# A hybrid retention and attention block: weight slabs requested one at a time, casts chained, one v-stage low half and the output pieces moved

## The chip, the cores and the metric

The kernel runs on one core of a Trainium2 chip. The metric is device time in microseconds (us) for one execution of the whole program. Engines are named as in the profile: PE multiplies matrices (PEld loads its weights), DVE and ACT work element by element, POOL does so too, SP issues most DMA transfers. Each engine runs its instructions in the order in which they stand; between engines and DMA queues, semaphores hold an instruction back until its data and its buffer are ready.

## The reference, cut to what matters

One layer over x of 1024 rows and 1024 columns, all in float32:

```python
h = rms_norm(x, ln1_g)
rq, rk, rv, rg, aq, ak, av, gate_a, gate_b = split(h @ w_in + b_in)

# A: retention, 4 heads, q and k of 128, v of 256, chunks of 128
ry = head_group_norm(retention_chunkwise(rotary(rq), rotary(rk), rv))
branch_a = (silu(rg) * ry) @ w_ret_out

# B: attention in a window of 128, 16 query heads of 64, 2 key heads, sinks
ay = sliding_window_sink_attention(rotary(aq), rotary(ak), av, sinks)
branch_b = ay @ w_attn_out

merged = sigmoid(gate_a) * branch_a + sigmoid(gate_b) * branch_b
x = x + merged @ w_out
h2 = rms_norm(x, ln2_g)
x = x + (silu(h2 @ w_gate) * (h2 @ w_up)) @ w_down
out = rms_norm(x, lnf_g)
```

The change touches how three parts of this are fed: the columns of `w_in` for `aq` and the gates, those for `rv`, and `ay` on its way to `w_attn_out`.

## The kernel before, in words

Every float32 product is done as three products of halves. A **high half** is a cast on ACT (`nc.scalar.copy`), the **low half** is what the cast leaves out, a subtraction on DVE; PE adds high×high, high×low and low×high in one PSUM bank. `split` (L132) makes both halves, its two instructions stand at L133 (ACT) and L136 (DVE). A weight so takes a way of four steps: a DMA brings a raw slab, ACT casts it, DVE subtracts, PE multiplies.

The program runs in stages, one after the other on PE: norm and keys and values of the attention (to about 43 us), the **units stage** (43 to 343), the **v stage** (343 to 423), the w stage (423 to 616), retention with the output projections, and the feed-forward part.

In the **units stage** the attention runs as 32 units: unit u is quad g = u // 8 (four query heads) and block b = u % 8 of 128 rows. The loop at L630 takes in each turn the transposes of unit i−2 (`u_transpose`), the scores of unit i (`u_scores`), some steps of filler products, and the values of unit i−2 (`u_values`). Scores go to a ring of two PSUM banks (`s`, two heads each); ACT copies one half of a bank to SBUF (L521), DVE puts the other half in (`copy_predicated`, L522) and takes the minimum (L524), and ACT does the exponentials (L532). The transposed probabilities are split into `ph` (ACT, L550) and `pl` (DVE, L551), from which DVE masks `qh` and `ql` (L558); the values take four products, the last with `ql` (L570).

The filler products come from `items`: QuadQ 0 and 1, Gate 6, QuadQ 2, Gate 7, QuadQ 3, and ten more gates. A QuadQ makes the queries of one quad: two raw slabs, two halves z of weights of 8 k-slabs, four products of 24 matmuls (`aq`), and behind each second one a **rotation** (L468 to L477: six rows on DVE, two casts on ACT, two low halves on DVE). The rotated rows go to DRAM by four stores and come back in another layout by four loads (`send_turned`, L488 and L490). The rotation's buffers are rings, `rab` of 3 and `st1`, `st2` of 1, free again when the stores have landed. A Gate has one raw slab and two products of 24 matmuls (`acc_g`), each followed by a tanh (L591) and a store (L592).

Raw slabs have a ring of two. `load_ahead` (L599) requests the next item's slabs when all of them fit: a QuadQ so waits until both slabs of the ring are handed out again. `prep` (L605) makes the halves of an item's weights, and `filling` (L611) calls it for the next item at step 0 of a gate and at step 23 of a quad; a quad's second half z comes when its own products begin. SP and PE keep the order in which the code issues (`in_order`); on ACT and DVE the tile framework's scheduler sets it in this stage.

In the **v stage** seven products of quarter matrices make `rv` (a scheme that saves one of eight). Each has four k-slabs, 28 in all, prepared by `vprep(n)` (L765: cast and low half of one slab, tiles `vP`) and multiplied by `vproduct` (12 matmuls, L790). ACT, DVE and PE keep the code's order here. Ahead of the products DVE builds sums of quarters of h in `vacc` (`quad`, an addition at L721, and `vsub`, L724; 1024 columns each), in two turns c; the slabs 0 and 1 are prepared within turn 0, slab 2 behind turn 1, and slab n+3 ahead of product n.

The w stage does the like for pairs of columns (L1004 loop over `wseq`, products at L945; P7 adds to the bank of P6 behind the copy of L950). From product (8, "P6") on, each turn also does one piece of `split_ay` (L980): the sum of a pair in the attention's output and its halves, for the output projection.

## Time and profile before

| what | us |
|---|---|
| median of three runs | 1563.3 |
| lowest and highest | 1561.29, 1566.37 |
| the profiled execution | 1562.72 |
| its span in the trace | 1560.9 |
| units stage | 43 to 342.8 |
| v stage | 342.8 to 423 |
| w stage | 423 to 616 |

In the rows of a timeline the columns are: start, duration, engine, line and operation, what is written and read, the shape, how many, and in brackets the idle time ahead with what ended it. The ends of matmuls are modelled, so a row of PE reaches into the next; starts are what counts. In the rows of a window come the stretch, its length, the busy time of each engine with its count, the granted clock of PE (1.00 is full speed), the share of the DMA engines and GB/s.

### The profile page before, as it was taken

The numbers are of one execution on the slowest core, as the hardware profiler recorded it, in microseconds if no ns is written. First come the engines' busy times: TensorE is split into PE (matmuls) and PEld (weight loads), VectorE is DVE, ScalarE is ACT, GpSimd is POOL, SyncE is SP. The second block draws the span as 40 slices with busy tenths as digits, with TensorE's granted clock in tenths as the row PEclk, the third lists the DMA queues.
The fourth block names the chain that finished last, engine by engine and source line by source line (L and its number), as shares of the span: only waits on it lengthen the run. The fifth ranks groups of instructions, "written<-read, shape, count | busy, mean of one in ns | idle before, by whom it ended". The sixth has DMA issues, their size and how long they took to land.

```text
span 1560.9 us, 20542 instructions
## 1 busy us (share of the span) xinstructions
PE 1541.4 (99%) x7323; PEld 1288.5 (83%) x7323; DVE 1027.7 (66%) x1670; ACT 704.0 (45%) x1436; POOL 387.1 (25%) x336
## 2 busy tenths in 40 slices
PE   9989999999999999999999999999999999999998
PEld 8868888878888888888888888888888888888886
DVE  6577777788567666978557788444444444678756
ACT  6355677743234334545223365333333333344445
POOL 2001110000054441000021124655555555100001
PEclk9999999999999999999999999999999999999999
DMA  6674545330475455654555302333333333863233
GB/s 216 194 204 145 166 150 194 129 121 32 147 194 169 138 166 201 236 170 159 178 189 203 148 1 99 112 103 103 108 110 104 101 101 102 304 241 94 88 106 123
DMA packets 156355, 228.34 MB, mean 146 GB/s; under 512 B 10011, under 2 KB 82525, under 8 KB 155998
## 3 DMA queue, kind: packets, MB, share of 16 engines
q1 hardware_dynamic: 154972, 222.85, 43.6%
q0 software_dynamic: 1280, 4.20, 0.8%
q8 instruction: 57, 0.93, 0.2%
q14 instruction: 44, 0.36, 0.1%
q10 hardware_dynamic: 2, 0.00, 0.0%
HBM read 152.29 MB, written 69.99 MB: 142 GB/s over the span
## 4 chain that ended last, share of the span: by engine, by line
PE 94%; DVE 3%; ACT 1%; issue 1%; DMA 1%; SPq 0%; POOL 0%; POOLq 0%; DVEq 0%
PE fA L1651 15%; PE fB L1651 8%; PE dA L1953 7%; PE wA L945 7%; PE dxP L1953 6%; PE fC L1651 4%; PE wB L945 3%; PE wo L1485 3%; PE acc_g L160 3%; PE acc_g L161 3%; PE acc_g L162 3%; PE va L790 3%; PE woP L1485 2%; PE vP L790 2%; PE aq L160 2%; PE aq L162 2%
## 5 line engine op out<-in xcount | busy, mean ns | idle before, releaser
L1953 PE MATMUL dA<-dwP,daP 128*128 128x512 f32 x528 | 120.6, 389 | 0.0
L1953 PEld LDWEIGHTS dA<-dwP,daP 128*128 128x128 f32 x528 | 99.0, 188 | 20.7 <-DVE dwP L136 0.2
L1953 PE MATMUL dxP<-dwP,daP 128*128 128x512 f32 x396 | 90.2, 389 | 0.0
L1953 PEld LDWEIGHTS dxP<-dwP,daP 128*128 128x128 f32 x396 | 74.3, 188 | 15.4
L160 PE MATMUL acc_g<-h,wh_g 128*128 128x512 f32 x192 | 75.3, 392 | 0.0
L161 PE MATMUL acc_g<-h,wh_g 128*128 128x512 f32 x192 | 74.9, 390 | 0.0
L162 PE MATMUL acc_g<-h,wl_g 128*128 128x512 f32 x192 | 74.8, 389 | 0.0
L508 POOL COPY sc<-nsink 128x4 f32<-128x4 f32 x32 | 10.5, 327 | 246.3 <-issue 71.1
L1726 POOL TENSOR_TENSOR xf<-xf 128x512 f32<-128x512 f32 x40 | 61.2, 1530 | 31.2 <-issue 28.9
L532 ACT ACTIVATE sc<-sc,nm 128x129 f32<-128x129 f32 x128 | 50.1, 394 | 35.1 <-DVE nm L524 25.8
L1657 POOL TENSOR_TENSOR xf<-xf 128x512 f32<-128x512 f32 x33 | 47.3, 1435 | 58.9 <-ACT xf L1659 26.9
L160 PE MATMUL aq<-h,wh_aq 128*128 128x512 f32 x128 | 51.1, 399 | 6.4 <-ACT wh_aq L425 6.4
L136 DVE TENSOR_TENSOR dwP<-wd,dwP 128x512 fp32r<-128x512 f32 x77 | 52.8, 686 | 5.3 <-ACT dwP L133 5.1
L1858 POOL TENSOR_TENSOR rs_f<-tot,mhalf 128x1 f32<-128x1 f32 x8 | 4.8, 606 | 205.4 <-DVE tot L1855 205.4
L133 ACT CAST dwP<-wd 128x512 fp32r<-128x512 f32 x77 | 47.4, 616 | 9.3 <-PE dA L1953 7.1
L160 PE MATMUL acc_bb<-ay,wh_bb 128*128 128x512 f32 x128 | 51.1, 399 | 0.0
L162 PE MATMUL aq<-h,wl_aq 128*128 128x512 f32 x128 | 50.8, 397 | 0.0
L161 PE MATMUL aq<-h,wh_aq 128*128 128x512 f32 x128 | 50.7, 396 | 0.0
L659 POOL TENSOR_TENSOR wr_wp<-wr_wp 128x512 f32<-128x512 f32 x10 | 15.7, 1570 | 140.4 <-DVE w0P L136 121.7
L133 ACT CAST daP<-daP 128x512 fp32r<-128x512 f32 x42 | 26.0, 621 | 54.3 <-PE dxP L1953 26.7
L162 PE MATMUL acc_bb<-ay,wl_bb 128*128 128x512 f32 x128 | 50.1, 391 | 0.0
L161 PE MATMUL acc_bb<-ay,wh_bb 128*128 128x512 f32 x128 | 50.1, 391 | 0.0
(845 smaller groups left out, 4353.2 us busy)
## 6 DMA issues: line engine op xcount, KB each, us to landing
act_d<-xf SPq DMA_DIRECT2D x77, 256.0 KB, 2.1
daP<-act_d SPq DMA_DIRECT2D x21, 512.0 KB, 3.6
q<-q_d SPq DMA_DIRECT2D x32, 256.0 KB, 4.7
wr_daP<-act_d SPq DMA_DIRECT2D x14, 512.0 KB, 3.8
wr_g<-in_w_in SPq DMA_DIRECT2D x12, 512.0 KB, 5.4
tb_d<-tb SPq DMA_DIRECT2D x24, 256.0 KB, 4.8
wd<-in_w_ffn_down SPq DMA_DIRECT2D x6, 1024.0 KB, 13.3
wr_f<-in_w_ffn_gate SPq DMA_DIRECT2D x11, 512.0 KB, 3.9
```

The costliest lines, as they stand in the source:

```text
L133: nc.scalar.copy(hi, raw)
L136: return nc.vector.tensor_tensor(out=lo, in0=raw, in1=f32(hi), op=ALU.subtract)
L160: nc.tensor.matmul(pt, hi[:, k, :], xh, start=(k == 0), stop=False)
L161: nc.tensor.matmul(pt, hi[:, k, :], xl, start=False, stop=False)
L162: nc.tensor.matmul(pt, lo[:, k, :], xh, start=False, stop=(k == 7))
L532: nc.scalar.activation(sc[:, j, 0:P + 1], sc[:, j, 0:P + 1], AF.Exp, scale=-1.0, bias=nm[:, j:j + 1], accum_out=den[:, j:j + 1])
L790: nc.tensor.matmul(vbanks[pr][tt], x_[:, c], w[:, u, :], start=(fresh and k + z == 0), stop=(k == 3 and z == 2), skip_group_check=not fresh)
L945: nc.tensor.matmul(pt, o[:, w, k, :], v, start=(first and k + z == 0), stop=(k == 3 and z == 2), skip_group_check=not first)
L1485: nc.tensor.matmul(bank, v[:, q + u, k, c], w[y][:, k % 2, :], start=(first and z == 0), stop=(last and z == 2), skip_group_check=not tracked)
L1651: nc.tensor.matmul(pt, o[:, w, k, :], v, start=(first and n == 0), stop=(n == 11), skip_group_check=not first)
L1726: nc.gpsimd.tensor_tensor(out=o, in0=a, in1=b, op=op)
L1953: nc.tensor.matmul(banks[tt], a[:, u, c], w[:, v, :], start=(fresh and f + z == 0), stop=(f == NP - 1 and z == 2), skip_group_check=not fresh)
```

## The change

It has four parts. `QuadQ.load` requests one raw slab at each call, and `load_ahead` goes through a list of single slabs, so that a quad's first slab is requested as soon as one place of the ring is free. `tie` chains instructions in the order of the code, without a semaphore: the casts of weights and of `ph` on ACT, and the low halves of weights and `pl` on DVE; the scheduler can't put one ahead of the other any more. The next item's weights come at step 4 of a gate that a quad follows, and the first rotation's stores of a quad are sent at the next `prep` (for quad 0 still at once). In the v stage `vprep(2)` moves into turn 1, ahead of its last three rows of DVE. The pieces of `split_ay` begin two products earlier, at (7, "P3").

```diff
--- before.py
+++ after.py
@@ -118,6 +118,13 @@
                                       reason="in_order")
                 prev[i.engine] = i.name
 
+
+    def tie(chain, op):
+        if chain:
+            tc.add_manual_dep(op.ins, chain[-1].name,
+                              mybir.DependencyInfo(mybir.DependencyClass.NoSync, mybir.DependencyReason.DATA),
+                              reason="tie")
+        chain.append(op.ins)
 
     def raw_slab(shape, name):
         return ring.tile([P] + shape, F32, tag="wr", name=f"wr_{name}", bufs=2)
@@ -404,6 +411,8 @@
                 ak_evac(q // 2, kb[q // 2])
                 av_evac(q // 2, vb[q // 2])
 
+        acts, vecs = [], []
+
         class QuadQ:
             raws, size = 2, 2
 
@@ -411,19 +420,20 @@
                 self.g, self.raw, self.w = g, [], []
 
             def load(self):
-                for kk in range(2):
-                    raw = raw_slab([4, 256], f"aq{self.g}{kk}")
-                    nc.sync.dma_start(raw, w_in[kk * 512:kk * 512 + 512, C_AQ + self.g * 256:C_AQ + self.g * 256 + 256]
-                                      .rearrange("(k p) n -> p k n", p=P))
-                    self.raw.append(raw.rearrange("p k (j z e) -> p k z j e", j=4, z=2, e=32))
+                kk = len(self.raw)
+                raw = raw_slab([4, 256], f"aq{self.g}{kk}")
+                nc.sync.dma_start(raw, w_in[kk * 512:kk * 512 + 512, C_AQ + self.g * 256:C_AQ + self.g * 256 + 256]
+                                  .rearrange("(k p) n -> p k n", p=P))
+                self.raw.append(raw.rearrange("p k (j z e) -> p k z j e", j=4, z=2, e=32))
 
             def prep(self):
                 z = len(self.w)
                 self.w.append(hl_tiles([8, P], f"aq{self.g}{z}"))
                 for kk in range(2):
                     hi, lo = (t[:, kk * 4:kk * 4 + 4, :].rearrange("p k (j e) -> p k j e", e=32) for t in self.w[z])
-                    nc.scalar.copy(hi, self.raw[kk][:, :, z])
-                    nc.vector.tensor_tensor(out=lo, in0=self.raw[kk][:, :, z], in1=f32(hi), op=ALU.subtract)
+                    tie(acts, nc.scalar.copy(hi, self.raw[kk][:, :, z]))
+                    tie(vecs, nc.vector.tensor_tensor(out=lo, in0=self.raw[kk][:, :, z], in1=f32(hi),
+                                                      op=ALU.subtract))
 
             def products(self):
                 return quad_q(self.g, self.w)
@@ -441,7 +451,9 @@
 
             def prep(self):
                 self.w.append(hl_tiles([8, P], f"g{self.n}"))
-                split(self.raw, *self.w[0])
+                hi, lo = self.w[0]
+                tie(acts, nc.scalar.copy(hi, self.raw))
+                tie(vecs, nc.vector.tensor_tensor(out=lo, in0=self.raw, in1=f32(hi), op=ALU.subtract))
 
             def products(self):
                 return gate(self.n, self.w[0])
@@ -476,7 +488,7 @@
                 nc.scalar.activation(s1.bitcast(F32R), b, AF.Copy)
                 nc.vector.tensor_tensor(out=b.bitcast(F32R), in0=b, in1=s1, op=ALU.subtract)
                 turns.append((q_d[2 * g + half], (a, s1, s2, b), Bt[:, jb:jb + 4, c]))
-                if half == 0:
+                if g == 0 and half == 0:
                     send_turned()
                 yield
 
@@ -547,8 +559,8 @@
             for j in range(4):
                 nc.tensor.transpose(pt[:, j * P:(j + 1) * P], sc[:, j, 0:P], ident)
             ph, pl = (w1.tile([P, 512], F32R, tag=t, bufs=1, name=f"{t}{g}{b}") for t in ("ph", "pl"))
-            nc.scalar.copy(ph, pt)
-            nc.vector.tensor_tensor(out=pl, in0=pt, in1=f32(ph), op=ALU.subtract)
+            tie(acts, nc.scalar.copy(ph, pt))
+            tie(vecs, nc.vector.tensor_tensor(out=pl, in0=pt, in1=f32(ph), op=ALU.subtract))
             phs[u] = [(vev[:, b // 2], ph, pl)]
             if b > 0:
                 mk = amask[:, P:2 * P].rearrange("p (o s) -> p o s", o=1).to_broadcast([P, 4, P])
@@ -596,11 +608,12 @@
         items = [QuadQ(0), QuadQ(1), Gate(order[0]), QuadQ(2), Gate(order[1]), QuadQ(3)] + [Gate(n) for n in order[2:]]
         loaded = [0, 0]
 
+        asked = [it for it in items for _ in range(it.raws)]
+
         def load_ahead():
-            while loaded[0] < len(items) and loaded[1] + items[loaded[0]].raws <= 2:
-                items[loaded[0]].load()
-                loaded[1] += items[loaded[0]].raws
-                loaded[0] += 1
+            while asked and loaded[1] < 2:
+                asked.pop(0).load()
+                loaded[1] += 1
 
         def prep(it):
             it.prep()
@@ -610,13 +623,14 @@
 
         def filling(n):
             it = items[n]
-            late = it.size == 2
             while len(it.w) < it.size:
                 prep(it)
             send_turned()
+            at = 23 if it.size == 2 else 4 if n + 1 < len(items) and items[n + 1].size == 2 else 0
             for k, _ in enumerate(it.products()):
-                if k == (23 if late else 0) and n + 1 < len(items):
+                if k == at and n + 1 < len(items):
                     prep(items[n + 1])
+                    send_turned()
                 yield
 
         load_ahead()
@@ -815,10 +829,11 @@
                     vprep(1)
                 quad(x2_, 11)
                 vsub(x2_, x1, x2_)
+                if c:
+                    vprep(2)
                 vsub(x3, x4, x2_)
                 quad(x4, 12)
                 vsub(x4, x4, x2_)
-            vprep(2)
             for n in range(28):
                 pr, k = VORDER[n // 4], n % 4
                 if n + 3 < 28:
@@ -1004,7 +1019,7 @@
         for i, (j, pr) in enumerate(wseq):
             wprep_to(i + 3)
             wnow[0] = i
-            piece = i - wseq.index((8, "P6"))
+            piece = i - wseq.index((7, "P3"))
             if piece >= 0:
                 split_ay(piece, True)
             wproduct(j, pr)
```

**SP, units stage.** The first place is SP's queue around the weights of quad 2. The names: `q_d` is the DRAM tensor of the rotated rows, `q100`, `st210`, `st110`, `q110` are quad 1's first half, `q0` is where the loads bring them, `wr_aq20` and `wr_aq21` are quad 2's two raw slabs, `wr_g6` is that of gate 6. Before:

```order
L488 DMA q_d_72<-st101_805 128x512
L488 DMA q_d_72<-q011_803 128x512
L490 DMA q0_670<-q_d_72 32x4x512 x4
L488 DMA q_d_72<-q100_858 128x512
L488 DMA q_d_72<-st210_888 128x512
L488 DMA q_d_72<-st110_887 128x512
L488 DMA q_d_72<-q110_885 128x512
L490 DMA q0_670<-q_d_72 32x4x512 x4
L416 DMA wr_aq20_963<-in_w_in 128x4x256
L416 DMA wr_aq21_965<-in_w_in 128x4x256
```

Now:

```order
L502 DMA q0_670<-q_d_72 32x4x512 x4
L450 DMA wr_g6_823<-in_w_in 128x8x128
L425 DMA wr_aq20_825<-in_w_in 128x4x256
L500 DMA q_d_72<-q001_770 128x512
L500 DMA q_d_72<-st201_806 128x512
L500 DMA q_d_72<-st101_805 128x512
L500 DMA q_d_72<-q011_803 128x512
L502 DMA q0_670<-q_d_72 32x4x512 x4
L425 DMA wr_aq21_957<-in_w_in 128x4x256
L500 DMA q_d_72<-q100_860 128x512
```

The request of quad 2's first slab stands right behind that of gate 6, ahead of the last stores of quad 0; the second stands ahead of the stores of quad 1's first half, which were ahead of both.

**ACT, units stage.** The second place is ACT and DVE around the casts of quad 2's weights. `sc03` and `s030` are the scores of quad 0, block 3, `xy00` the output of block 0, `wh_aq20` the high halves of quad 2's weights for z = 0, `wh_aq21` those for z = 1, `tb60` the tanh of gate 6. Before, ACT, up to and behind the four casts:

```order
L532 ACTIVATE sc03_1134,den03_1137<-sc03_1134,nm03_1136 128x129 x2
L573 COPY xy01_1190<-pv01_1185 128x512
L532 ACTIVATE sc03_1134,den03_1137<-sc03_1134,nm03_1136 128x129 x2
L550 CAST ph02_1198<-pT02_1193 128x512
L521 COPY sc04_1206<-s040_1210 128x2x128
L521 COPY sc04_1206<-s041_1220 128x2x128
L532 ACTIVATE sc04_1206,den04_1209<-sc04_1206,nm04_1208 128x129 x4
L425 CAST wh_aq20_1045<-wr_aq20_963 128x512
L425 CAST wh_aq21_1233<-wr_aq20_963 128x512
L425 CAST wh_aq20_1045<-wr_aq21_965 128x512
L425 CAST wh_aq21_1233<-wr_aq21_965 128x512
L573 COPY xy02_1269<-pv02_1264 128x512
```

Now, ACT, around the first two casts:

```order
L533 COPY sc02_1057<-s020_1061 128x2x128
L434 CAST wh_aq20_1093<-wr_aq20_825 128x512
L533 COPY sc02_1057<-s021_1071 128x2x128
L544 ACTIVATE sc02_1057,den02_1060<-sc02_1057,nm02_1059 128x129 x4
L603 ACTIVATE tb60_1108<-acc_g6_0_1041,bhalf_89 128x512
L585 COPY xy00_1118<-pv00_1115 128x512
L434 CAST wh_aq20_1093<-wr_aq21_957 128x512
L562 CAST ph01_1126<-pT01_1121 128x512
L471 ACTIVATE q111_1019<-aq111_967,bcol_88 128x512
L533 COPY sc03_1134<-s030_1138 128x2x128
L533 COPY sc03_1134<-s031_1148 128x2x128
L603 ACTIVATE tb61_1182<-acc_g6_1_1111,bhalf_89 128x512
```

The two casts for z = 0 stood behind the exponentials of block 4 and now stand before the second score copy of block 2 and before `ph01`; those for z = 1 follow later, ahead of the exponentials of block 4.

**DVE, units stage.** DVE in the same place; `st211`, `q101`, `st111`, `q111` are the rotation of quad 1's second half. Before:

```order
L537 TENSOR_TENSOR sc02_1063<-sc02_1063,rd02_1087 128x4x128
L468 TENSOR_TENSOR st211_1022<-q101_957,atab_178 128x512
L471 TENSOR_TENSOR q101_957<-q101_957,atab_178 128x512
L469 TENSOR_TENSOR st111_1021<-q111_1019,atab_178 128x512
L551 TENSOR_TENSOR pl01_1127<-pT01_1121,ph01_1126 128x512
L470 TENSOR_TENSOR st211_1022<-st211_1022,st111_1021 128x512
L472 TENSOR_TENSOR q111_1019<-q111_1019,atab_178 128x512
L558 SCALAR_TENSOR_TENSOR qh01_1130<-amask_180,ph01_1126 128x512
L473 TENSOR_TENSOR q111_1019<-q111_1019,q101_957 128x512
L558 SCALAR_TENSOR_TENSOR ql01_1132<-amask_180,pl01_1127 128x512
L522 COPY_PREDICATED sc03_1134<-amask_180,s030_1138 128x2x128
L475 TENSOR_TENSOR st211_1022<-st211_1022,q101_957 128x512
```

Now:

```order
L549 TENSOR_TENSOR sc02_1057<-sc02_1057,rd02_1081 128x4x128
L435 TENSOR_TENSOR wl_aq20_1094<-wr_aq21_957,wh_aq20_1093 128x512
L563 TENSOR_TENSOR pl01_1127<-pT01_1121,ph01_1126 128x512
L480 TENSOR_TENSOR st211_1022<-q101_951,atab_178 128x512
L481 TENSOR_TENSOR st111_1021<-q111_1019,atab_178 128x512
L483 TENSOR_TENSOR q101_951<-q101_951,atab_178 128x512
L482 TENSOR_TENSOR st211_1022<-st211_1022,st111_1021 128x512
L484 TENSOR_TENSOR q111_1019<-q111_1019,atab_178 128x512
L570 SCALAR_TENSOR_TENSOR qh01_1130<-amask_180,ph01_1126 128x512
L485 TENSOR_TENSOR q111_1019<-q111_1019,q101_951 128x512
L570 SCALAR_TENSOR_TENSOR ql01_1132<-amask_180,pl01_1127 128x512
L534 COPY_PREDICATED sc03_1134<-amask_180,s030_1138 128x2x128
```

The low half for z = 0 of the second slab (that of the first stands three rows further ahead) is ahead of `pl01`, and the rotation's rows, of which three stood ahead of `pl01`, follow behind it.

**DVE, v stage.** The third place is DVE ahead of the first products of v; `vP12` and `vP13` are the third and the fourth slab's tiles, `s23` a half of the sums. Before:

```order
L721 TENSOR_TENSOR vacc_3678<-h0_111 128x2x512
L724 TENSOR_TENSOR vacc_3678<-vacc_3678 128x2x512 x2
L721 TENSOR_TENSOR vacc_3678<-h1_112 128x2x512
L724 TENSOR_TENSOR vacc_3678<-vacc_3678 128x2x512
L136 TENSOR_TENSOR vP12_3718<-wv_2571,vP12_3718 128x512
L136 TENSOR_TENSOR vP13_3721<-wv_2571,vP13_3721 128x512
L663 TENSOR_TENSOR s23_3673<-vacc_3678,s23_3673 128x1024
L136 TENSOR_TENSOR vP20_3738<-wv_2571,vP20_3738 128x512
```

Now:

```order
L735 TENSOR_TENSOR vacc_3678<-h0_111 128x2x512
L738 TENSOR_TENSOR vacc_3678<-vacc_3678 128x2x512
L143 TENSOR_TENSOR vP12_3715<-wv_2571,vP12_3715 128x512
L738 TENSOR_TENSOR vacc_3678<-vacc_3678 128x2x512
L735 TENSOR_TENSOR vacc_3678<-h1_112 128x2x512
L738 TENSOR_TENSOR vacc_3678<-vacc_3678 128x2x512
L143 TENSOR_TENSOR vP13_3721<-wv_2571,vP13_3721 128x512
L677 TENSOR_TENSOR s23_3673<-vacc_3678,s23_3673 128x1024
```

`vP12` moved ahead of three rows of `vacc`; `vP13` kept its place.

## The prediction

> **What bounds the kernel now.** I read the page's first part, then the waits of PE, then PE's rows around each wait.

> ```profile
> PE 1541.4 (99%) x7323; PEld 1288.5 (83%) x7323; DVE 1027.7 (66%) x1670; ACT 704.0 (45%) x1436; POOL 387.1 (25%) x336
> ```

> PE is busy for 99% of the span, the next engine, DVE, for 66%. So an edit of ACT, DVE or SP changes the time only by what PE waits, or by the clock at which PE runs. The waits of PE, by line and releaser (us in total, times, longest):

> ```profile
> PE aq L160 <- ACT wh_aq L425: 6.4, 1, 6.4
> PE va L790 <- DVE vP L136: 2.2, 1, 2.2
> ...
> PE wA L945 <- ACT u L950: 0.7, 1, 0.7
> PE wA L945 <- DVE w2P L136: 0.4, 1, 0.4
> ```

> Two waits behind the start are over 1 us, and both lie where the change works: quad 2's first product in the units stage, and the third k-slab of the v stage. Here is the first, on PE:

> ```profile
> 105.23 0.28 PE L516 MATMUL s<-kst,q 128*128 128x256 f32 x1
> 105.35 0.28 PE L517 MATMUL s<-kst,q 128*128 128x256 f32 x1
> 112.05 0.80 PE L160 MATMUL aq<-h,wh_aq 128*128 128x512 f32 x1 [6.42 <-ACT wh_aq L425]
> ...
> 116.64 0.39 PE L161 MATMUL aq<-h,wh_aq 128*128 128x512 f32 x1
> 116.87 0.39 PE L162 MATMUL aq<-h,wl_aq 128*128 128x512 f32 x1
> ```

> Score rows start 0.12 apart, so the next product was due at 105.47 and came at 112.05: **6.58 lost**. Ten steps lie between 112.05 and 116.64 (the nine rows left out are of the same form): 4.59. At the pitch of the last two rows, 0.23, they take 2.27 (0.2267 each, from 25 rows below): another **2.32 lost**. The windows say why (us, busy time of PE, PEld, DVE, ACT, POOL, then the granted clock):

> ```profile
> 106.00:112.00 6.00, 0.00 (x0) 0.00 (x0) 4.44 (x11) 3.24 (x14) 0.42 (x1) 0.81 0.94 281
> 112.00:116.00 4.00, 3.95 (x9) 2.84 (x10) 2.83 (x5) 1.56 (x3) 0.00 (x0) 0.50 0.37 114
> 353.00:355.00 2.00, 2.00 (x6) 1.63 (x5) 2.00 (x4) 0.08 (x1) 0.00 (x0) 0.50 0.00 0
> 604.00:605.00 1.00, 0.51 (x2) 0.46 (x3) 0.97 (x2) 0.96 (x2) 0.00 (x0) 1.00 0.15 56
> ```

> Behind the 6.42 wait the clock is 0.50 for some 4 us, behind the 2.21 wait in v (at 353) as well, behind the 0.68 wait at 604 it stays 1.00. A long wait so costs twice: itself, and half speed behind it. What held quad 2's weights back stands on ACT and SP:

> ```profile
> 111.39 2.16 ACT L425 CAST wh_aq<-wr_aq 128x512 fp32r<-128x512 f32 x4
> ```
> ```profile
> 93.10 0.97 SPq L416 DMA_DIRECT2D wr_aq<-in_w_in  x2
> ```

> The slabs were asked for at 93.1, 18 us ahead; both halves' four casts simply stood behind unit 4's exps in ACT's order. The time is lost to order, not to a transfer.

> **Part A: slabs one by one, casts tied.** The order shows the first cast ahead of unit 2's second score copy and the second behind unit 0's output copy, each long before PE needs them, and their two low halves likewise on DVE. This removes 6.58 + 2.32 = **8.90**.

> It adds no instruction, but two low halves of 0.6 us come into a stretch where DVE was full:

> ```profile
> 97.19 0.59 ACT L573 COPY xy<-pv 128x512 f32<-128x512 f32 x1 [0.45 <-PE pv L570]
> 97.68 0.59 ACT L550 CAST ph<-pT 128x512 fp32r<-128x512 f32 x1
> ```
> ```profile
> 98.30 0.69 DVE L551 TENSOR_TENSOR pl<-pT,ph 128x512 fp32r<-128x512 f32 x1
> ...
> 101.31 0.68 DVE L558 SCALAR_TENSOR_TENSOR ql<-amask,pl 128x512 fp32r<-128x512 f32 x1
> ...
> 103.78 0.43 DVE L522 COPY_PREDICATED sc<-amask,s 128x256 f32<-128x256 uint32 x1
> ```
> ```profile
> 103.85 0.39 PE L570 MATMUL pv<-ql,vdf 128*128 128x512 f32 x1
> ```

> Now the second cast follows the copy of 97.19 in place of the row at 97.68, and takes about as long as that row, to 98.3. DVE, in order, waits for it, does wl_aq to 98.95, and then pl, five rotation rows, qh and a sixth rotation row: eight ahead of ql, at the pitch of that stretch, 0.60 (98.30 to 101.31 is five steps, 3.01; the old order had done three of the rotation rows ahead of pl). So ql begins near 103.8 and ends near 104.48, 2.5 later than before, where PE's fourth value product is due at 103.85: a wait of about 0.68 with the hand-over. Then come the first score bank's copy, two rotation rows, a reduction and the second bank's copy, the row of 103.78: some 2.2 together, to 106.7. PE's second pair of unit 4's scores, which takes that second bank, is due at 105.67 (its rows began at 105.23 − 2 × 0.12 = 104.99, and 0.68): about 1.07 more. With the restart of PE (0.16 above: 6.58 against 6.42) that is **A′ = 1.9**. Its bounds: not below nothing, since PE had no wait there that could go; zero if ACT and DVE run 1 us ahead of my reckoning; 4.2 if the waits trip the half clock (1.9 plus 2.32). I take 1.9, as each wait is near the 0.68 at 604 that left the clock alone.

> The other moves of A are covered. wh_aq's second pair is needed two products of 24 rows later (some 11 us of filler and units), and stands in ACT ahead of unit 4's exps. Quad 3's casts come 50 us later in the same pattern, and the same count leaves ql there some 1.5 us ahead of its product. On SP the second slab's request stands ahead of quad 1's first stores; it waits for gate 6's low half, done before the stores' data are. For quad 2 it delays the stores, priced under the rivals.

> **Part B: v's third low half moved.** PE, DVE and ACT in v:

> ```profile
> 342.80 5.86 PE L790 MATMUL va<-vP,h 128*128 128x512 f32 x25
> 350.87 7.13 PE L790 MATMUL va<-vP,h 128*128 128x512 f32 x23 [2.21 <-DVE vP L136]
> 357.83 4.47 PE L790 MATMUL vP<-vP,h 128*128 128x512 f32 x19
> ```
> ```profile
> 345.20 2.48 DVE L724 TENSOR_TENSOR vacc<-vacc 128x1024 f32<-128x1024 f32 x2
> ...
> 350.13 1.28 DVE L136 TENSOR_TENSOR vP<-wv,vP 128x512 fp32r<-128x512 f32 x2
> ```
> ```profile
> 343.88 0.61 ACT L133 CAST vP<-wv 128x512 fp32r<-128x512 f32 x1
> 412.39 10.88 PE va L790 x48
> ```

> The last row is of the chain of waits: 48 products in 10.88, so 0.2267 each. Product 26 was due at 342.80 + 25 × 0.2267 = 348.47 and came at 350.87: 2.40 lost. The next 23 took 357.83 − 350.87 = 6.96 in place of 5.21: 1.75 lost to the 0.50 clock. **B = 4.15.** The third low half goes ahead of three of DVE's 1.23 us rows: it starts behind the first of the two rows at 345.20, at 346.45, and ends near 347.1, well before 348.47; its cast is ahead of 343.88 on ACT. But the fourth low half stays behind the same work, so it ends where it ended, near 351.4 (second row of the 350.13 group). PE needs it after the third slab's 12 products and one of its own: 348.47 + 12 × 0.2267 = 351.19. So **B′**: 0.28 of wait and 0.16 of restart, 0.4 remain; bounds 0 and 2.2 (0.44 plus 1.75, if that wait tripped the clock).

> [...]

> **Part C: output pieces two products earlier.** Casts, sums and low halves of the attention output, about 0.6 us each on ACT and DVE, move up by two products of the w stage; their tensors were loaded long before.

> ```profile
> 600.94 2.88 PE L945 MATMUL wA<-s,w9P 128*128 128x512 f32 x12
> 604.49 3.02 PE L945 MATMUL wA<-s,w9P 128*128 128x512 f32 x12 [0.68 <-ACT u L950]
> ```

> The wait there is of the copy of P6's bank, which P7 continues: 600.94 + 12 × 0.2267 = 603.66, so the copy cannot start sooner. The wait stays whatever the pieces do. A piece that came between would add one 0.59 row of ACT at most, a lighter queue could give back 0.3 of it: from −0.3 to 0.7, and I take 0, as PE shows no other wait after 604.

> **Sum.** −8.90 + 1.9 − 4.15 + 0.4 + 0 = −10.75. The profiled execution took 1562.72 (span 1560.9, and 1.8 around it), the median of the three runs is 1563.3. 1562.72 − 10.75 = **1552.0**.

> **The rivals.** *R1, no new waits*: the order is fixed but ACT and DVE run ahead; all 13.05 gained, 1549.7. For it: 1 us would do. Against: DVE's rows stand without a gap.

> *R2, a new wait trips the half clock*: 0.68 and 1.07 lie within 2 us of each other, and 0.44 in v comes alone. 1.75 in v gives 1553.7; with 2.32 in the units stage too, 1556.1. Against: the row at 604.

> *R3, the slow rows behind v's wait aren't due to it*, and stay: B is 2.40, and the sum gives 1552.0 + 1.75 = 1553.7. Against: they begin just behind the wait, as at 112. [...]

> *R4, the casts are early in the order but not in time*: DVE, or a slab that lands late, holds PE as before. Only B is gained: 1562.72 − 4.15 + 0.4 = 1559.0. Against: the requests come earlier than the one of 93.10.

> *R5, slower: quad 2's stores stuck on SP.* The store rows now stand behind the second slab's request, which waits for gate 7's low half.

> ```profile
> 140.35 1.22 DVE L136 TENSOR_TENSOR wl_g<-wr_g,wh_g 128x1024 fp32r<-128x1024 f32 x1
> ```
> ```profile
> 147.23 0.67 ACT L459 ACTIVATE q<-aq,bcol 128x512 f32<-128x512 f32 x1
> ```
> ```profile
> q_d<-st SPq DMA_DIRECT2D x16, 256.0 KB, 2.9
> ```

> Gate 7's half ends at 141.57, the request takes 0.5, the stores then issue from 142.1 to 143.8 and land by 146.7 (2.9 by the page's DMA rows). ACT's evacuation into the freed buffer came at 147.23, so 0.5 is left. If the stores land later, ACT and DVE, both in order, stop with unit exps behind them, and PE waits for scores. To be slower by 0.3% it must eat the 10.75 and 4.7 more, 15.5 in two quads (2 and 3): some 8 us each, so landing near 155. Each would be like the wait of 6.42 with its slow clock: 1552.0 + 2 × 8.9 = **1569.8**.

> **How the numbers follow.** Forecast 0.52 (1552.0); R1 0.16 (1549.7); R2 0.16 (1553.7 to 1556.1); R3 0.04 (1553.7); R4 0.08 (1559.0); R5 0.04 (1569.8). A measurement of this kernel can tell about 0.3%, 4.7 us, from no change, so the bounds are 1558.6 and 1568.0. Faster: forecast, R1, R2 and R3, 0.88; R4 is within, 0.08; R5 slower, 0.04. The range leaves R4 and R5 out: from 1548.5 (R1 less 1.2 for the spread between runs, whose lowest lies 2.0 under the median) to 1557.5 (R2's end, which holds the bounds of A′ and B′, and 1.4 for the median's 0.6 over the profiled run and the spread; part C's bounds lie inside).

> **What would show it.** In the changed kernel's waits of PE the 6.4 and 2.2 must be gone, with the 0.7 near 604 kept. Step A′ is right if, between 103 and 108, value products wait for ql and scores for the copy of a score bank, under 1 us each, with the clock at 1.00; and B′ if one wait of 0.3 for a low half stands 37 products into v, with the clock at 1.00 through the next 4 us. A wait of several us near quad 2's or quad 3's first product, a clock of 0.50 in either place, or ACT evacuations that wait for stores would make the prediction wrong.

## The result, and the profile after

| | before | changed |
|---|---|---|
| median, us | 1562.3 (4 runs, 1560.84 to 1566.37) | 1554.03 (4 runs, 1553.4 to 1555.02) |
| profiled execution, us | 1562.72 | 1554.35 |
| its span, us | 1560.9 | 1552.6 |

The ratio is 0.9944, 95% interval 0.9923 to 0.9964: faster by half a per cent. A second measurement (e10 below) gave 0.9943 (0.9927 to 0.9958). The forecast was 1552.0, the range 1548.5 to 1557.5.

PE's waits in the changed kernel, the same view as before (us in total, times, longest):

```profile
PE s L528 <- DVE sc L534: 0.9, 1, 0.9
PE wA L960 <- ACT u L965: 0.7, 1, 0.7
PE pv L582 <- DVE ql L570: 0.5, 1, 0.5
PE wA L960 <- DVE w2P L143: 0.3, 1, 0.3
```

The 6.4 and the 2.2 are gone, the 0.7 is kept, and two new waits stand at the two places that the prediction names. PE's rows there:

```profile
105.30 0.40 PE L582 MATMUL pv<-qh,vdf 128*128 128x512 f32 x1
106.16 0.50 PE L582 MATMUL pv<-ql,vdf 128*128 128x512 f32 x1 [0.47 <-DVE ql L570]
...
107.29 0.28 PE L529 MATMUL s<-kst,q 128*128 128x256 f32 x1
108.47 0.36 PE L528 MATMUL s<-kst,q 128*128 128x256 f32 x1 [0.90 <-DVE sc L534]
```

The ql product was due at 105.53 and comes at 106.16 (0.63); the second pair of scores was due at 107.41 and comes at 108.47 (1.06). DVE shows why, with the wait for the second cast and no gap from there to the bank's copy at 107.89:

```profile
100.00 0.69 DVE L435 TENSOR_TENSOR wl_aq<-wr_aq,wh_aq 128x512 fp32r<-128x512 f32 x1 [2.17 <-ACT wh_aq L434]
...
105.42 0.69 DVE L570 SCALAR_TENSOR_TENSOR ql<-amask,pl 128x512 fp32r<-128x512 f32 x1
...
107.89 0.43 DVE L534 COPY_PREDICATED sc<-amask,s 128x256 f32<-128x256 uint32 x1
```

In v, PE runs through:

```profile
338.31 11.34 PE L804 MATMUL va<-vP,h 128*128 128x512 f32 x48
349.48 6.74 PE L804 MATMUL vP<-vP,h 128*128 128x512 f32 x29
```

The first 48 products take 349.48 − 338.31 = 11.17, where they took 15.03 (342.80 to 357.83). At 0.2267 each they need 10.88, so 0.29 is left, 0.24 of it in the two steps behind the 37th product, where the fourth slab's low half is needed.

Where the time went follows from matching starts on PE, since its order is the same in both:

| stretch | forecast | measured | from |
|---|---|---|---|
| start to quad 0's first product | 0 | +1.68 | 42.93 to 44.61 |
| quad 2's first product, A and A′ | −7.0 | −7.04 | shift +1.68 to −5.36 |
| rest of the units stage | 0 | +0.87 | shift −5.36 to −4.49 |
| first 48 products of v, B and B′ | −3.75 | −3.86 | 15.03 to 11.17 |
| all behind | 0 | 0.0 | shift −8.35 to the end |

The sum, −8.35, is the difference of the profiled executions (−8.37). The medians lie 8.3 apart as well; what the start and the clock took in the executions that were not profiled is not known. Two rows were not foreseen: 1.68 at the start, and 0.87 in the last units. The latter is below the size that the view of waits lists; PE's rows of a late unit's values show it:

```profile
313.50 0.39 PE L582 MATMUL pv<-ph,vev 128*128 128x512 f32 x1
313.72 0.39 PE L582 MATMUL pv<-pl,vev 128*128 128x512 f32 x1
314.21 0.49 PE L582 MATMUL pv<-qh,vdf 128*128 128x512 f32 x1
314.81 0.50 PE L582 MATMUL pv<-ql,vdf 128*128 128x512 f32 x1
```

In the unit's values at 321.06 to 321.74 these starts are 0.22 to 0.23 apart; here they are 0.49 and 0.60 apart, so 0.26 and 0.37 are lost, with no idle row printed.

### The profile page after: what moved, and what is told of

It reads as the page before. It is cut to its first block, busy times and chain, and to the rows that moved or that the text cites. A ratio compares the mean times of both kernels' runs of the same rounds, so it can differ in the third digit from the quotient of the medians.

```text
span 1552.6 us, 20526 instructions
## 1 busy us (share of the span) xinstructions
PE 1541.1 (99%) x7323; PEld 1287.7 (83%) x7323; DVE 1024.6 (66%) x1670; ACT 704.4 (45%) x1436; POOL 388.0 (25%) x336
## 4 chain that ended last, share of the span: by engine, by line
PE 93%; DVE 3%; ACT 2%; issue 1%; POOL 0%; DMA 0%; POOLq 0%; DVEq 0%; ACTq 0%
PE fA L1666 15%; PE fB L1666 8%; PE dA L1968 7%; PE wA L960 7%; PE dxP L1968 6%; PE fC L1666 4%; PE wB L960 3%; PE va L804 3%; PE wo L1500 3%; PE woP L1500 2%; PE vP L804 2%; PE acc_g L167 2%; PE acc_g L168 2%; PE acc_g L169 2%; PE aq L167 2%; PE aq L168 2%
## 6 DMA issues: line engine op xcount, KB each, us to landing
act_d<-xf SPq DMA_DIRECT2D x77, 256.0 KB, 2.1
q<-q_d SPq DMA_DIRECT2D x32, 256.0 KB, 4.6
tb_d<-tb SPq DMA_DIRECT2D x24, 256.0 KB, 4.9
wd<-in_w_ffn_down SPq DMA_DIRECT2D x6, 1024.0 KB, 13.3
```

## The experiments

Below, "the shift" is PE's start of a unit's values against the profiled run before, each run counted from its own first product of quad 0, so that differences of the start drop out. For the changed kernel it is −7.04 behind quad 2's first product and −6.17 at the start of v.

**e1, v's part alone.** Before, with the third low half moved:

```diff
                 vsub(x2_, x1, x2_)
+                if c:
+                    vprep(2)
                 vsub(x3, x4, x2_)
                 quad(x4, 12)
                 vsub(x4, x4, x2_)
-            vprep(2)
```

> The kernel before, with only v's third low half moved ahead of three rows of DVE. If the wait of 2.21 us in v and the 0.50 clock behind it are one cost, both go: the 48 products of v's first two... product groups take about 11.2 us instead of 15.0, the wait of 6.4 us in the units stage stays, and the time falls by 3.9 us, to about 1558.5. If the slow rows behind the wait have another cause, they stay and the time falls by 2.1 us only.

Measured: the 48 products took 11.18, a gain of 3.85; the time 1560.15 against 1562.76, ratio 0.998 (0.9971 to 0.999). In the profile the rest was lost in places that the edit does not touch: 0.67 as the slow stretch behind the 6.4 us wait lasted 10.24 in place of 6.83 us, and 1.66 behind v, most of it in waits for w2P in the w stage. The medians are 2.61 apart. That is between 3.85 and the 2.24 that this edit gains against an execution of before without slow rows in v (e8 below).

**e2, the units' part alone.** The changed kernel with `vprep(2)` behind turn 1 again and the pieces at (8, "P6").

> The changed kernel with the v stage's and the w stage's parts undone: slabs one by one, chained casts, stores behind them. Expected from the changed kernel's trace: the 6.4 us wait is gone, waits of 0.5 and 0.9 us for ql and for a score bank stand at 106 to 108, small waits of 0.9 us together stand in the last units, and the 2.2 us wait in v with its slow rows is back: 7.0 less 0.9, so 6.1 us below before, about 1556.5. If the pieces of the attention output in the w stage were worth anything, the time differs from that by more than the runs do.

Measured: 1555.81, ratio 0.9955 (0.994 to 0.997). The shift is −7.05 behind quad 2's product and −6.18 at v, as in the changed kernel. The surprise is in v, where the wait of before is back but not its slow rows:

```profile
336.10 5.88 PE L804 MATMUL va<-vP,h 128*128 128x512 f32 x25
344.17 5.51 PE L804 MATMUL va<-vP,h 128*128 128x512 f32 x23 [2.19 <-DVE vP L143]
349.52 0.84 PE L804 MATMUL vP<-vP,h 128*128 128x512 f32 x3
```

The 23 products take 5.35 here and took 6.96 before, behind the same wait. e8 takes this up.

**e3, without the chain.** The changed kernel, with `tie` adding no order:

```diff
-        if chain:
+        if False:
```

> The changed kernel without the chain (tie adds no order). Theory 1, the chain is what keeps the weights' casts early: without it the casts fall behind the exponentials again, the 6.4 us wait returns and the time is about 1560. Theory 2, the scheduler puts the casts early anyway once the slabs are requested ahead of quad 1's first stores, and the chain only makes DVE wait for the second cast: the 6.4 us wait stays away, the waits for ql and for the score bank shrink from 1.7 us to under 0.4, unit 24's exponentials are not late by 1.0 us, the waits in the last units go (0.9 us), and the time is about 1551.8, some 2 us below the changed kernel.

Measured: 1552.77, ratio 0.9935 (0.9918 to 0.9951). Theory 2 holds at quad 2: the shift is −8.51, so what is newly lost there shrank from 1.87 to 0.42, and the last units lose next to nothing (0.04). But a wait of 0.7 for a score bank came at quad 3 (0.92 of shift). The chain so costs 1.47 at quad 2 and 0.87 in the last units, and saves 0.92 at quad 3.

**e4, one condition alone.** Before, with:

```diff
-                if half == 0:
+                if g == 0 and half == 0:
                     send_turned()
```

> The kernel before with one condition changed: the stores of a quad's first rotation are sent at once for quad 0 alone, for the others at the next call that comes anyway. Slabs are still requested as a pair, nothing is chained. Theory 1 (single slabs or the chain are needed): the 6.4 us wait stays, the time is that of before. Theory 2 (the request only had to stand ahead of quad 1's first stores in SP's queue, since the scheduler puts a cast where it reckons the slab to land): the casts go ahead of unit 4's exponentials, the 6.4 us wait and its slow rows go (8.9 us), at most 0.3 us of new waits come at 104 to 106, and the time is 8.6 us below before, about 1554.

Measured: 1557.09, ratio 0.996 (0.9945 to 0.9975). The shift behind quad 2's product is −8.51: this one condition removes the 6.4 us wait, with neither single slabs nor a chain. At quad 3 it then loses 2.21, which the expectation of 1554 did not have. Since quad 2's stores now come later, DVE waits for one to land before it can refill the rotation's buffer, and PE for the ql behind it:

```profile
143.64 0.69 DVE L468 TENSOR_TENSOR st<-q,atab 128x512 f32<-128x512 f32 x1 [1.12 <-DMA q_d<-st]
```
```profile
151.17 0.50 PE L570 MATMUL pv<-ql,vdf 128*128 128x512 f32 x1 [1.31 <-DVE ql L558]
```

**e5, single slabs alone.** Before, with the new `QuadQ.load` and `load_ahead`.

> The kernel before with slabs requested one by one and nothing else. Quad 2's first slab is requested ahead of quad 1's first stores, the second still behind them. In the order its first cast stands early, the second behind unit 4's exponentials. Theory 1 (single slabs make the gain): the 6.4 us wait is gone. Theory 2 (a cast goes where the scheduler reckons its slab to land): PE does the first slab's 12 products at 105.5 and then waits some 3 to 4 us for the second cast, at about 111.5; the wait shrinks and does not go.

Measured, one run: 1560.13, 3.9 below the run before beside it, and theory 2. PE does twelve products from 106.51 and waits for the second slab's cast.

```profile
109.02 0.39 PE L162 MATMUL aq<-h,wl_aq 128*128 128x512 f32 x1
112.56 0.50 PE L160 MATMUL aq<-h,wh_aq 128*128 128x512 f32 x1 [3.16 <-ACT wh_aq L425]
```

The shift is −3.4. Half of the wait went, the other half stayed with the slab whose request still stood behind the stores.

**e6, the chain alone.** Before, with `tie` on the same instructions.

> The kernel before with the chain alone: slabs as a pair, behind quad 1's first stores. The chain keeps the first two casts ahead of ph01, so the 6.4 us wait goes by it alone as well; DVE waits for the second cast, and PE waits 1 to 2 us for ql and for a score bank, as in the changed kernel. If the small waits of the last units (0.9 us) come from the chain, they are there too; if they come from the single slabs or from step 4, they are not.

Measured, one run: 1570.17, 6.1 above the run before beside it. The expectation missed. The view of PE's waits has a new row in place of the old one:

```profile
PE pv L581 <- ACT ph L561: 8.5, 2, 6.1
```

The chain keeps `ph01` behind the weights' casts. The scheduler still puts those late, behind the rotation's casts, and now the unit's own cast waits with them. An earlier place would have gained little at quad 2: ACT's rows show that the second cast began only when its slab had landed, with `ph01` behind it:

```profile
101.58 0.62 ACT L434 CAST wh_aq<-wr_aq 128x512 fp32r<-128x512 f32 x1 [0.25 <-DMA wr_aq<-in_w_in]
102.11 0.58 ACT L561 CAST ph<-pT 128x512 fp32r<-128x512 f32 x1
```

So PE waits 6.12 for `ph01` there, and with the slow rows behind it this costs what the old wait cost: the shift behind quad 2's product is +0.16. What the time is longer by comes later, 5.27 at quad 3 (a wait of 2.34 for the `ph` of a unit behind casts whose slabs had long landed, then slow rows) and 0.87 in the last units. In v the wait of 2.2 stayed.

**e7, v's third low half only one row ahead.** The changed kernel, `vprep(2)` behind `quad(x4, 12)`.

> The changed kernel with v's third low half moved back by two of DVE's three rows: it ends 2.5 us later, so PE waits some 1.0 us in v. If a wait of that size is enough for the half clock, the 48 products take 11.2 + 1.2 + 1.7 = 14.1 us; if not, 12.4 us with the clock at 1.00.

Measured, one run: 1554.79, with a wait of 1.0 in v, the 48 products in 12.19, no low clock. Against the 11.17 of the changed kernel the wait of 1.0 cost 1.02 here.

**e8, the kernel before again.** No edit.

> The kernel before, once more under the profiler. The waits of 6.4 and 2.2 us stand where they stood. Theory 1 (a wait of 2.2 us halves the clock): 0.50 for 3.4 us behind the wait in v, as before. Theory 2 (the clock is judged in fixed stretches of 3.41 us, and only a stretch that holds nearly all of the wait counts): the 0.50 behind the 2.2 us wait may be absent, as in the run of the units part alone; where it is there, its start lies a whole number of 3.413 us from the start of the low stretch at 110, and every low stretch lasts 3.41 us or a multiple.

Measured, one run: 1563.14, with the same two waits, 6.4 and 2.2, but no slow rows in v. PE's row and the window behind the wait:

```profile
350.78 5.51 PE L790 MATMUL va<-vP,h 128*128 128x512 f32 x23 [2.19 <-DVE vP L136]
```
```profile
351.00:355.00 4.00, 4.00 (x18) 3.27 (x18) 4.00 (x6) 0.63 (x1) 0.00 (x0) 1.00 0.00 0
```

The 48 products took 13.42 (342.71 to 356.13), against 15.03 in the other execution of the very same program. Theory 1 is out, and theory 2 holds in the main: the section on the hardware has the stretches, and how much of each wait fell into one.

**e9, two edits that the runs left standing.** Before, with:

```diff
-                if half == 0:
+                if g != 1 and half == 0:
                     send_turned()
...
                 vsub(x2_, x1, x2_)
+                if c:
+                    vprep(2)
                 vsub(x3, x4, x2_)
                 quad(x4, 12)
+                if c:
+                    vprep(3)
                 vsub(x4, x4, x2_)
-            vprep(2)
...
-                if n + 3 < 28:
+                if 3 < n + 3 < 28:
```

> The kernel before with two edits only: the stores of a first rotation wait for the next call for quad 1 alone (quads 0, 2 and 3 send at once, as before), and v's third and fourth low halves are made ahead of three and of one of DVE's rows. No chain, no single slabs, pieces as before. If the gain of the units stage needs only the request of quad 2's slabs ahead of quad 1's first stores, the stage shrinks by 8.5 us against its own start; with quad 2's stores sent at once, the 2.2 us that the run with stores behind for all quads lost at quad 3 do not come, nor the 0.9 us of the last units. In v the 48 products take 10.9 to 11.0 us. Together some 12.5 us below before, about 1550, and 3 to 4 us below the changed kernel. If the chain is needed at quad 3, a wait of 0.7 to 1.3 us at 146 to 154 remains.

Measured: 1551.61 (5 runs, 1550.0 to 1552.62), ratio 0.9926 (0.9914 to 0.9939), 3.0 below the changed kernel measured beside it (1554.65; each of the five runs here is below each of the five there). The shift is −8.51 behind quad 2's product and still −8.51 at v, and the 48 products take 10.91:

```profile
335.98 11.07 PE L790 MATMUL va<-vP,h 128*128 128x512 f32 x48
346.89 2.43 PE L790 MATMUL vP<-vP,h 128*128 128x512 f32 x10
```

**e10, the changed kernel again.** No edit.

> The changed kernel on the same chip, for comparison: 1554 us, with the waits of 0.5 and 0.9 us at 104 to 108 and the small ones of the last units where they were, since they come from the order; the start of PE's first products and the landings in the w stage may differ by 1 to 2 us from run to run.

Measured: 1554.65 (5 runs, 1552.66 to 1556.53). All waits of the units stage came again at the same size; the shift is −7.07 and −6.15 at v.

**e11, the pieces undone.** The changed kernel, pieces at (8, "P6").

> The changed kernel with the pieces of the attention output starting at (8, P6) again. If they only fill idle rows of ACT and DVE, the w stage from its product at 5.4 us to the output projection's first differs by nothing but the 0.6 us steps of the w2P waits, and the 0.7 us wait for the copy of the bank stays: within 0.7 us of the changed kernel.

Measured, one run: 1555.03. From the w stage's first product to the output projection's first it took 193.5; the changed kernel took 193.1 and 192.6 in its two profiles, the kernel before 193.2 and 194.4. The pieces make no difference that can be told from this spread, and the wait of 0.68 stands in all.

## Why the prediction was right, point by point

**Part A and A′** came out as worked: −8.90 and +1.87 (forecast +1.9), with ql and the score bank late by 0.63 and 1.06 (forecast 0.68 and 1.07) and 0.18 in smaller steps behind them (forecast 0.16), the clock at 1.00. What the prediction did not separate is which of the three edits does it. It said that the time is lost to order, not to a transfer; the runs show where that order comes from. In the order before, the casts stood late because the requests stood behind quad 1's first four stores and four loads. Moving the requests ahead of these is enough (e4); with one slab ahead half the wait goes (e5); pinning the casts without moving the requests makes it worse (e6). The prediction's "18 us ahead" counts from the request; in the kernel before the two slabs landed at 100.6 and 102.0, behind those stores and loads. So the casts at 111.39 were late by order, as it says, but a cast pinned ahead of `ph01` at 97.7 has no data yet, which e6 ran into. The changed kernel asks for the second slab at 87.3 and has it at 91.0. The move of a gate's preparation to step 4 was not run by itself; e9 does without it. That the scheduler reckons a cast's place from when its slab would land is inferred from these orders, not read from it.

**Part B and B′** came out as worked, 3.86 against 3.75, the remaining wait with its restart 0.29 against 0.4. Its 2.40 is there in every profile of before. Its 1.75 is not: six profiles have this wait, and the 48 products take 15.0 in four of them (before, e4, e5, e6) and 13.42 in two (e2, e8), without the half clock. "A long wait so costs twice" was true of the profiled run and of the other three that took 15.0, not of the two that took 13.42. That the 1.75 came as forecast was therefore luck: against the run e8, v's part would have gained 13.42 − 11.17 = 2.25.

**Part C** was nothing that can be told from the spread, as forecast, and the wait for the bank's copy stayed, by the reason given: it is PE's own.

**What failed** is the sentence that the other moves of A are covered. Quad 3's casts were; the gates' were not. With the chain, a gate's low half at the end of quad 2 goes behind `pl`; it now stands between the last of unit 24's four score rows, which itself fell behind ql, and that unit's reciprocal. DVE in the kernel before, where it stood ahead of all four:

```profile
256.64 1.23 DVE L136 TENSOR_TENSOR wl_g<-wr_g,wh_g 128x1024 fp32r<-128x1024 f32 x1 [0.46 <-ACT wh_g L133]
257.79 0.34 DVE L529 CUSTOM_DVE_ANT_0 sc<-s,amask,nsink 128x128 f32<-128x128 f32 x1
...
263.15 0.17 DVE L535 RECIPROCAL rd<-den 128x4 f32<-128x4 f32 x1
```

And in the changed kernel:

```profile
256.18 0.69 DVE L570 SCALAR_TENSOR_TENSOR qh<-amask,ph 128x512 fp32r<-128x512 f32 x1
256.78 0.69 DVE L570 SCALAR_TENSOR_TENSOR ql<-amask,pl 128x512 fp32r<-128x512 f32 x1
257.38 0.35 DVE L541 CUSTOM_DVE_ANT_0 sc<-s,amask,nsink 128x128 f32<-128x128 f32 x1
257.65 0.08 DVE L541 DVE_READ_ACCUMULATOR2_ANT nm<- 128x1 f32 x1
257.65 1.22 DVE L456 TENSOR_TENSOR wl_g<-wr_g,wh_g 128x1024 fp32r<-128x1024 f32 x1
258.79 0.17 DVE L547 RECIPROCAL rd<-den 128x4 f32<-128x4 f32 x1
```

With PE's shift the reciprocal of 263.15 would be at 257.80: it is 0.99 late. From there ACT and DVE need about 7.4 us for a unit (reciprocals at 258.79 and 310.57, seven units) and PE about 7.1 (values at 264.38 and 307.15, six units). The lead shrinks, and the missing 1 us comes due in units 29 to 31 as 0.87. In every profile with the chain this order, the 1 us and the loss are there (changed kernel, e2, e6, e7, e10, e11), in every one without it they are not. That the loss at the end comes from this one low half, and not from another instruction of the chain, is argued from the rows; no run moved it alone.

**The start's 1.68** is not of the change. Quad 0's first product comes at 44.6 in the changed kernel, e4, e9, e10 and e11, and at 42.2 to 42.9 in before, e1, e2, e3, e6, e7 and e8 (43.8 in e5): kernels with and without the change are in both groups. PE's pace in the first 13 us makes the difference. Here are the same 24 products in the changed kernel:

```profile
8.68 1.03 PE L276 MATMUL warm<-wk 128*128 128x128 bf16 x8
9.50 3.62 PE L229 MATMUL lnT<-ident,wk 128*128 128x128 f32 x16
```

And in e2, whose code is the same up to v:

```profile
7.08 0.62 PE L276 MATMUL warm<-wk 128*128 128x128 bf16 x8
7.54 2.60 PE L229 MATMUL lnT<-ident,wk 128*128 128x128 f32 x16
```

The first entry of the granted clock in the traces is full speed, from 12.8 to 13.3 us on in the five profiles that start at 44.6 and from 3.9 to 5.8 us on in the other eight. Ahead of it a trace has no entry (the view of windows prints 1.00 there), so that PE ran at the low clock until then is inferred from its pace: in the run before, the same 16 transposes took 3.59 from 7.42 on, with the clock at 0.50 from 7.38 to 10.78. With the 0.87 this start makes up the 2.4 by which the profiled execution lies above the forecast.

**The rivals.** R5's mechanism exists: DVE waits for the late stores (1.00 in the changed kernel at 141, 1.12 in e4). It costs PE nothing in the changed kernel and 2.21 in e4, far from the 8 that it was priced at. R2 did not come: the two new waits, 0.47 and 0.90, lie in one stretch of the clock (see the last section), and the clock stayed at 1.00. R3's sum did not come either; its premise was half right, as no profile has slow rows in v without the wait, but the wait alone does not make them (e2 and e8: 2.19, and the clock at 1.00). R4's mechanism, a slab that lands late behind an early place in the order, is what the second cast met in e6 (0.25 of idle time for its DMA).

## What to carry to other kernels

When a cast or a copy stands late on its engine though its data landed long ago, look at what stands ahead of its DMA's request in the issuing queue, before pinning the order: one moved store group did here what the pins did, without their price. A pin ties the pinned instruction to the lateness of all that is ahead of it, so pins belong only where the order was seen to be wrong. And a stage whose helpers run slower than PE hides a delay only as long as its lead lasts (here 7.4 us for a unit against PE's 7.1); look for the bill at the stage's end.

## What the runs showed of the hardware

Windows of the kernel before at the edges of the stretches in which its granted clock was low (the clock is the third number from the end):

```profile
7.00:8.00 1.00, 0.63 (x4) 0.59 (x4) 1.00 (x3) 0.00 (x0) 0.74 (x2) 0.69 1.05 379
10.00:11.00 1.00, 1.00 (x8) 1.00 (x7) 0.69 (x1) 1.00 (x3) 1.00 (x2) 0.61 1.06 415
109.00:110.00 1.00, 0.00 (x0) 0.00 (x0) 1.00 (x4) 0.16 (x1) 0.00 (x0) 0.89 1.04 363
352.00:353.00 1.00, 1.00 (x5) 0.77 (x4) 1.00 (x2) 0.00 (x0) 0.00 (x0) 0.56 0.00 0
355.00:356.00 1.00, 1.00 (x4) 0.73 (x4) 1.00 (x2) 0.54 (x1) 0.00 (x0) 0.73 0.00 0
```

In the run before, PE was idle from 106.37 to 109.78, all 3.41 us, and the clock was 0.50 behind that; it was idle for 2.27 of the next stretch, up to 112.05, and the clock stayed at 0.50; it ran from 113.19 to 116.60, and the clock was back at 1.00. In v 2.16 us of its idle time fell between 348.71 and 352.12, and the next stretch was slow. In e8, whose low stretch at the start began at 7.62 (the clock from 7 to 8 is 0.81), an edge fell at 348.95, the larger part of the wait was 1.83, and the clock was 1.00 from 351 to 355. In the changed kernel the clock next fell at 1549.32 (it is 0.66 from 1549 to 1550, PE's last product ended at 1545.7), which puts edges at 105.48 and 108.89: the waits of 0.47 and 0.90 lie between them, and the clock was 1.00 from 104 to 113.

So in these runs the clock was at half behind stretches with 2.16 and 3.41 us idle, and at full behind those with 1.83 and 1.37. The start does not fit: in the run before the clock fell at 7.38 behind 3.41 us in which PE's rows leave 0.33 idle (from 7.05 on). So idle time in the rows is not all that counted, and what else did is not shown.

The other spread between executions is in DMA landings: in the w stage the transfers `xw<-r` held DVE until 467.25 in the changed kernel (3.36 us of idle time) and 468.73 in e2, from the same place in both. What of such a delay reaches PE was not measured by itself; PE's listed wait for w2P is 0.34 in the changed kernel and 0.38 in the run before. Executions of one kernel side by side lie 1.6 us (the changed kernel, 4 runs) to 6.2 us (the kernel before, 15 runs beside e1) apart, so edits of 1 us were read here from PE's shift at a place, not from the total.
